# A new queue order for the FFN-up stretch of a one-core decoder layer (GpSimd transfer behind two products)

## The chip, the cores and the metric

One Trainium2 chip, one core. The metric is the device time in microseconds (us), the median of several runs. A profile is one execution of the same program with the hardware profiler on.

## What is computed

One decoder layer on 512 positions of width 1024, in fp32: two parallel mixers (sparse attention and gated DeltaNet), an output projection, a layer norm, a gated feed-forward network (FFN) with a width-3 causal convolution, and another layer norm. The change lies in the FFN alone:

```python
h = x @ w_up                       # 512 x 1024 @ 1024 x 5632, two branches of 2816 columns
h = causal_dwconv(h, conv_w)       # each column: its own 3 taps along the positions
a, b = split(h)                    # gate branch a, value branch b
f = (silu(a) * b) @ w_down         # 512 x 2816 @ 2816 x 1024
x = layer_norm(alpha * x + f)
```

## The kernel before

**Precision.** TensorE multiplies in fp32r, so every operand is split in two: a rounded copy `wh` (or `mh`, `sh`), made by ScalarE, and the rest `wl` = raw - `wh` (`ml`, `sl`), made by VectorE. A product is then three matmuls: `mh`·`wh`, `ml`·`wh`, `mh`·`wl`. For every weight block the way is therefore: a transfer into `raw` on SyncE's queue (SP), ScalarE's copy into `wh`, VectorE's subtraction into `wl`, TensorE's matmuls. `raw`, `wh` and `wl` have three buffers each.

**FFN-up** runs over 22 groups p of 128 columns, each with two branches (b = 0, the gate, and b = 1).
- A plain group (`plain`, lines 1553 to 1570) loads `raw` (L1557), splits it (L1561 ScalarE, L1562 VectorE), and runs matmuls of 512 columns into the PSUM tiles `pu0` and `pu1` (L1567).
- The seven odd groups 5, 7, ... 17 (`seven`, lines 1474 to 1539) replace eight half-size products by seven (a Strassen scheme) with matmuls of 256 columns (L1514) into `px` and `pz`, out of loads `raw` and `raw7` (L1492 to L1499; `raw7` has one buffer) and their splits (L1503 ScalarE, L1504 VectorE). Their results are joined in `wf0` and `wf1` by ScalarE (L1523, L1528, L1531, L1538) and VectorE (L1526, L1533, L1536).
- `gated` (L1541) then makes `fa0` or `fa1`: ScalarE takes `pu` or `wf` out with the last tap (L1544), VectorE adds the other two (L1547, twice). After it come tanh on ScalarE into `fth` (L1605), VectorE (L1606), and the product `fth` x `fa1` on GpSimd (L1607). Last, `fth` is split for FFN-down (ScalarE L1611 and L1618 into `pha`, VectorE L1612 and L1619 into `pla`), and sums of its halves are made (`sr`, VectorE L1613 and L1620 to L1622). `fth` has three buffers, `fa0` and `fa1` two each.

**FFN-down** uses the same scheme. The sums of `w_down` that it needs are made in DRAM by eight transfers that add to `wsum`, issued on GpSimd's queue by `sums` (L538), one or two after each of seven groups. They run beside FFN-up.

**What sets the order.** The program is written in a plain order, and every engine's queue is then put in the order of a table written out by hand, `QUEUES` (L138 to L343): for PE, DVE (VectorE), Activation (ScalarE), Pool (GpSimd) and SP a list of instruction numbers in the order in which that engine is to run them. `queues` (L346) ties each instruction to the one ahead of it. Each engine runs its list strictly in that order; an instruction that waits holds up all behind it.

Names below carry a number for each tile. `pu0_5920` and `pu1_5984` are those of group 8, `fth_5860` and `fth_5911` of groups 6 and 7. `px1_5939`, `pz1_5941`, `wf0_5942` and `wf1_5943` belong to group 9, `pu1_6220` to group 10, `px0_6175`, `pz1_6177` and `wf0_6178` to group 11, `pu0_6392` with `raw_6393` to group 12, and `raw7_6416` to group 13.

The lines that make and use the product and the splits around it:

```python
A.activation(acc, ps, AF.Copy, scale=w[:, 2:3])                                    # L1544
A.activation(hi, r, AF.Copy)                                                       # L1561
V.tensor_tensor(lo, r, hi.bitcast(F32), op=OP.subtract)                            # L1562
A.activation(th, g[0], AF.Tanh, scale=0.5)                                         # L1605
V.scalar_tensor_tensor(th, th, 1.0, g[0], op0=OP.add, op1=OP.mult)                 # L1606
G.tensor_tensor(th, th, g[1], op=OP.mult)                                          # L1607
A.activation(ph.j(j, bs), both, AF.Copy)                                           # L1618
i = G.dma_start(out=wsum[to], in_=src, **({"accum_op": OP.add} if add else {}))    # L538
```

Of the kernel before, what the change touches and what calls it, by code (L numbers as in the profile page):

```python
# [70 lines left out]
def layout(a):  # L71
# [149 lines left out]
2775-2778 2784-2785 2779 2786-2787 2780-2781 2794 2788-2790 2795-2797 2791 2798 2792 2799-2803 2806-2808 2804 2793  # L221
2809-2812 2805 2813-2829 2842-2843 2854 2844-2845 2830-2833 2846 2834 2847-2848 2835 2849-2850 2855 2851 2836 2856
2852 2857 2853 2837 2858 2838 2859-2860 2839-2841 2861-2868 2890 2869-2870 2878 2871-2872 2891 2873 2879 2874-2877
2880-2886 2892-2896 2902 2897-2899 2887 2900-2901 2888-2889 2903-2908 2914 2909 2915 2910 2916 2911 2917 2926
2912-2913 2918 2927 2919-2921 2928-2932 2938 2933-2934 2939 2922-2923 2940-2942 2924-2925 2943-2946 2935 2947 2936
2948 2937 2949-2956 2962 2957-2959 2963 2960-2961 2964-2967 2974 2968-2969 2986-2987 2970 2975-2978 2971 2988-2989
2972 2990 2973 2979-2985 2998 2991 2999 2992-2993 3000-3002 2994-2995 3003 2996 3004-3005 3010-3012 3006-3007 2997
3008-3009 3022 3013-3017 3023-3024 3018 3025 3019-3020 3034 3026 3035-3036 3021 3027-3029 3037-3038 3030-3031 3039
3032 3040 3046 3033 3041-3042 3047-3049 3043-3044 3058 3045 3050-3053 3059-3061 3054-3057 3062 3070 3063-3067 3071
3068 3072-3075 3082 3069 3076 3083 3077 3084 3078-3079 3094-3095 3080 3085 3096 3081 3086-3087 3097-3100 3088-3089  # L230
3101 3090-3093 3106-3109 3102-3105 3110-3114 3118-3123 3115-3117 3124 3130 3125-3126 3131-3138 3127-3128 3142
3139-3140 3143-3144 3141 3154 3129 3155 3145-3146 3166 3147 3156 3148 3157-3158 3149-3153 3167 3159-3160 3168-3170
# [73 lines left out]
1237 1249 1230 1250 1252 1255 1251 1257-1258 1243 1261 1260 1263-1264 1246 1265 1253 1267 1266 1268 1273 1254 1222
1256 1259 1278 1269 1279 1282 1271 1283 1270 1288 1272 1262 1274 1293 1289 1292 1284 1280 1276 1294-1295 1286 1290
# [35 lines left out]
145-146 144 147-155 157-172 156 173-186 188 190 192 194-201 187 202 191 193 203 189 204-205""",  # L343
}
# [1421 lines left out]
```

## Time and profile before

| | |
|---|---|
| median of 3 runs | 828.61 us (827.09 to 830.98) |
| the profiled execution | 827.81 us |
| its span, first to last instruction | 826.0 us (1.81 lie outside it) |
| TensorE (PE) busy | 803.1 us, 97% of the span |
| VectorE (DVE) busy | 630.6 us, 76% |
| ScalarE (ACT) busy | 432.1 us, 52% |
| GpSimd (POOL) busy | 192.7 us, 23% |
| mean granted clock of TensorE | 0.993 |
| DMA | 139.80 MB, mean 169 GB/s |

In a timeline a row gives the start, the duration, the engine, the line and the tile written and read; in square brackets stands how long the engine had been idle before it, and which instruction ended that. Matmuls overlap: the next starts well before the last one's end. FFN-up fills the span from some 490 to 740 us.

### The profile page before, as it was taken

The numbers are of one execution on the slowest core, as the hardware profiler recorded it, in microseconds if no ns is written. First come the engines' busy times: TensorE is split into PE (matmuls) and PEld (weight loads), VectorE is DVE, ScalarE is ACT, GpSimd is POOL, SyncE is SP. The second block draws the span as 40 slices with busy tenths as digits, with TensorE's granted clock in tenths as the row PEclk, the third lists the DMA queues.
The fourth block names the chain that finished last, engine by engine and source line by source line (L and its number), as shares of the span: only waits on it lengthen the run. The fifth ranks groups of instructions, "written<-read, shape, count | busy, mean of one in ns | idle before, by whom it ended". The sixth has DMA issues, their size and how long they took to land. (4 is left out here: it accounts for less than half of the span.)

```text
span 826.0 us, 12475 instructions
## 1 busy us (share of the span) xinstructions
PE 803.1 (97%) x4390; PEld 680.1 (82%) x4390; DVE 630.6 (76%) x1391; ACT 432.1 (52%) x965; POOL 192.7 (23%) x186
## 2 busy tenths in 40 slices
PE   9999999999999999999899999989999999999996
PEld 8788888788788888888787998878798888887884
DVE  5666689969678965555569969867788967888797
ACT  4452687774576764322354336544555644665641
POOL 0334716042265211332200112220101221100001
PEclk9999999999999999999999999999999999999998
DMA  8233326857245936546666697799348467566664
GB/s 280 85 112 110 100 62 203 164 184 155 75 128 137 192 91 153 153 128 153 242 237 207 233 200 244 170 238 212 108 141 280 141 145 187 164 198 215 187 206 152
DMA packets 53406, 139.80 MB, mean 169 GB/s; under 512 B 3936, under 2 KB 5088, under 8 KB 53088
## 3 DMA queue, kind: packets, MB, share of 16 engines
q1 hardware_dynamic: 36064, 92.88, 34.6%
q0 software_dynamic: 17280, 46.14, 24.5%
q8 instruction: 34, 0.56, 0.3%
q14 instruction: 28, 0.23, 0.1%
HBM read 136.91 MB, written 48.23 MB: 224 GB/s over the span
## 5 line engine op out<-in xcount | busy, mean ns | idle before, releaser
L494 PE MATMUL gps<-xh,wh 128*128 128x512 f32 x320 | 124.5, 399 | 2.6 <-ACT mt L1146 2.3
L497 PE MATMUL gps<-xh,wl 128*128 128x512 f32 x320 | 123.6, 397 | 0.0
L496 PE MATMUL gps<-xl,wh 128*128 128x512 f32 x320 | 123.4, 395 | 0.0
L1567 PE MATMUL pu<-mh,wh 128*128 128x512 f32 x208 | 80.8, 399 | 3.5 <-ACT wh L1561 3.5
L1567 PE MATMUL pu<-mh,wl 128*128 128x512 f32 x208 | 80.2, 399 | 1.8 <-DVE wl L1562 1.7
L1607 POOL TENSOR_TENSOR fth<-fth,fa 128x512 f32<-128x512 f32 x22 | 31.9, 1451 | 209.6 <-DVE fth L1606 146.8
L1567 PE MATMUL pu<-ml,wh 128*128 128x512 f32 x208 | 80.1, 397 | 0.0
L494 PEld LDWEIGHTS gps<-xh,wh 128*128 128x128 f32 x320 | 59.9, 188 | 14.1 <-issue 3.1
L497 PEld LDWEIGHTS gps<-xh,wl 128*128 128x128 f32 x320 | 60.2, 188 | 11.7 <-POOL wl L484 0.6
L496 PEld LDWEIGHTS gps<-xl,wh 128*128 128x128 f32 x320 | 60.2, 189 | 10.5
L484 DVE TENSOR_TENSOR wl<-raw,wh 128x512 fp32r<-128x512 f32 x66 | 46.9, 716 | 24.1 <-PE gps L497 13.2
L1469 ACT ACTIVATE wh<-raw 128x512 fp32r<-128x512 f32 x67 | 40.4, 627 | 38.7 <-DMA raw<-wsum 13.0
L1562 DVE TENSOR_TENSOR wl<-raw,wh 128x512 fp32r<-128x512 f32 x52 | 39.1, 754 | 22.2 <-ACT wh L1561 12.3
L1470 DVE TENSOR_TENSOR wl<-raw,wh 128x512 fp32r<-128x512 f32 x67 | 45.3, 705 | 13.7 <-ACT wh L1469 13.4
L1561 ACT ACTIVATE wh<-raw 128x512 fp32r<-128x512 f32 x52 | 32.7, 629 | 40.5 <-PE pu L1567 34.2
L1503 ACT ACTIVATE wh<-raw 128x512 fp32r<-128x512 f32 x49 | 30.8, 630 | 39.6 <-PE px L1514 13.7
L1547 DVE SCALAR_TENSOR_TENSOR fa<-pu,fcw,fa 128x511 f32<-128x511 f32 (+1 forms) x60 | 44.3, 745 | 8.7 <-ACT fa L1544 8.6
L1567 PEld LDWEIGHTS pu<-mh,wh 128*128 128x128 f32 x208 | 39.8, 192 | 10.1 <-ACT wh L1561 3.9
L1567 PEld LDWEIGHTS pu<-mh,wl 128*128 128x128 f32 x208 | 39.9, 192 | 9.8 <-DVE wl L1562 3.1
L480 ACT ACTIVATE wh<-raw 128x512 fp32r<-128x512 f32 x46 | 28.8, 627 | 35.3 <-PE gps L496 23.7
L484 POOL TENSOR_TENSOR wl<-raw,wh 128x512 fp32r<-128x512 f32 x30 | 40.4, 1347 | 24.0 <-DVE wh L482 9.4
L1567 PEld LDWEIGHTS pu<-ml,wh 128*128 128x128 f32 x208 | 39.8, 191 | 6.5
(498 smaller groups left out, 2229.6 us busy)
## 6 DMA issues: line engine op xcount, KB each, us to landing
raw<-in_wT SPq DMA_DIRECT2D x40, 512.0 KB, 3.6
raw<-in_up SPq DMA_DIRECT2D x37, 512.0 KB, 4.6
wsum<-in_down POOLq DMA_DIRECT2D x6, 2816.0 KB, 22.4
usum<-in_up POOLq DMA_DIRECT2D x6, 1792.0 KB, 16.0
raw<-wsum SPq DMA_DIRECT2D x20, 512.0 KB, 3.9
raw<-in_down SPq DMA_DIRECT2D x15, 512.0 KB, 3.8
osum<-in_wo POOLq DMA_DIRECT2D x6, 1024.0 KB, 11.3
wsum<-wsum POOLq DMA_DIRECT2D x2, 2816.0 KB, 14.6
```

What stands on the lines that cost most here:

```text
L484: eng.tensor_tensor(wl, r, wh.bitcast(F32), op=OP.subtract)
L494: i = PE.matmul(ps, wh[k], mh_(k), start=(k == 0), stop=False)
L496: PE.matmul(ps, wh[k], ml_(k), start=False, stop=False)
L497: PE.matmul(ps, wl[k], mh_(k), start=False, stop=(k == n - 1))
L1469: A.activation(hi, raw[:, i], AF.Copy)
L1470: V.tensor_tensor(lo, raw[:, i], hi.bitcast(F32), op=OP.subtract)
L1503: E("uh", 10 * p + i, "A").activation(hi, r, AF.Copy)
L1547: V.scalar_tensor_tensor(acc[:, n:], ps[:, :S - n], w[:, i:i + 1], acc[:, n:], op0=OP.mult, op1=OP.add)
L1561: A.activation(hi, r, AF.Copy)
L1562: V.tensor_tensor(lo, r, hi.bitcast(F32), op=OP.subtract)
L1567: q = PE.matmul(ps, w[:, j], x[:, k, :], start=k == 0 and i == 0, stop=k == KD - 1 and i == 2, skip_group_check=True)
L1607: G.tensor_tensor(th, th, g[1], op=OP.mult)
```

## The change

No line of the program changes and no instruction is added or removed. The table `QUEUES` is made anew for all five queues in the stretch from about 545 to 700 us. In the Pool and SP tables:

```diff
     "Pool": ...
-133-134 111 135-138 140 139 141 150 142 151 143-145 157 146 148-149 160 147 152 163 153 156 154-155 158-159 161-162
-165-166 164 167-168 170-171 169 172-181""",
+133-134 111 135-138 140 139 141 150 142 151 143-145 157 146 148-149 160 147 152 163 153 156 155 154 158-159 161-162
+165 164 167 166 168 170-171 169 172-181""",
-    "SP": """0-7 17 8-9 15 25 10 12 11 13-14 19 18 16 20-22 24 23 26-75 81 78 77 82 79 83 76 84 80 85-129 132 130-131 133-143
+    "SP": """0-7 17 8-9 15 25 10 12 11 13-14 19 18 16 20-22 24 23 26-75 81 78 77 82 79 83 76 84 80 85-115 118 116-117 119-123 125
...
```

On SP three short loads of `raw` (L1499) move one or two places ahead of loads of `raw7`, and one L1496 load moves two places ahead. The tables of PE, DVE and Activation differ in many places of the stretch; the ones that matter below are these.

GpSimd's queue, all of its difference (`fth` products and `wsum` transfers):

```order
 L1607 TENSOR_TENSOR fth_5675<-fth_5675,fa1_5671 128x512
 L1607 TENSOR_TENSOR fth_5911<-fth_5911,fa1_5907 128x512
+L1607 TENSOR_TENSOR fth_5860<-fth_5860,fa1_5856 128x512
 L538 DMA wsum0_100<-in_down 1408x1x512
-L1607 TENSOR_TENSOR fth_5860<-fth_5860,fa1_5856 128x512
 L1607 TENSOR_TENSOR fth_6096<-fth_6096,fa1_6092 128x512
 L1607 TENSOR_TENSOR fth_6147<-fth_6147,fa1_6143 128x512
...
 L1607 TENSOR_TENSOR fth_6383<-fth_6383,fa1_6379 128x512
 L1607 TENSOR_TENSOR fth_6619<-fth_6619,fa1_6615 128x512
-L538 DMA wsum3_103<-wsum2_102 1408x512
 L1607 TENSOR_TENSOR fth_6568<-fth_6568,fa1_6564 128x512
 L1607 TENSOR_TENSOR fth_6804<-fth_6804,fa1_6800 128x512
+L538 DMA wsum3_103<-wsum2_102 1408x512
```

The transfer into `wsum0` now comes behind both products instead of between them, and the one into `wsum3` behind two more products.

ScalarE's queue after the tanh of group 7, at about 549 us (place A below), first as it is before, then as changed:

```order
L1605 ACTIVATE fth_5911<-fa0_5903 128x512
L1618 ACTIVATE pha_5439<-fth_5911 128x2x256
L1544 ACTIVATE fa0_5980<-pu0_5920,fcw_324 128x512
L1561 ACTIVATE wh_6159<-raw_6157 128x512
L1611 ACTIVATE pha_5439<-fth_5860 128x256
L1544 ACTIVATE fa1_6092<-pu1_5984,fcw_324 128x512
```

```order
L1605 ACTIVATE fth_5911<-fa0_5903 128x512
L1544 ACTIVATE fa0_5980<-pu0_5920,fcw_324 128x512
L1618 ACTIVATE pha_5439<-fth_5675 128x2x256
L1538 ACTIVATE wf0_5942<-px1_5939 128x256
L1544 ACTIVATE fa1_6092<-pu1_5984,fcw_324 128x512
L1561 ACTIVATE wh_6159<-raw_6157 128x512
```

The split of `fth_5911` no longer stands ahead of the weight copy `wh_6159`, and four other copies do. Of these, `fa1_6092` goes into the buffer of `fa1_5907`, which GpSimd's product `fth_5911` reads. On VectorE's queue the sum `wf1_5943` (L1536), which frees `pz` for the matmuls of about 566 us (place B), stood behind `wl_6260`; changed, it stands here:

```order
L1606 SCALAR_TENSOR_TENSOR fth_5911<-fth_5911,fa0_5903 128x512
L1562 TENSOR_TENSOR wl_6160<-raw_6157,wh_6159 128x512
L1620 TENSOR_TENSOR sr0a_5441<-fth_5860,fth_5911 128x256
L1547 SCALAR_TENSOR_TENSOR fa0_5980<-pu0_5920,fcw_324,fa0_5980 128x511
L1536 TENSOR_TENSOR wf1_5943<-wf1_5943,pz1_5941 128x256
L1504 TENSOR_TENSOR wl_6183<-raw7_6180,wh_6182 128x512
```

It moved thirteen places ahead. At about 579 us (place C) TensorE goes from group 10 to group 12, with half-size products of group 11 between. Its queue there, first as it is before, then as changed:

```order
L1514 MATMUL pz1_6177<-sh3_5460,wl_6340 128x256
L1514 MATMUL px0_6175<-mh_4006,wl_6359 128x256
L1567 MATMUL pu0_6392<-mh_4006,wh_6395 128x512
L1567 MATMUL pu0_6392<-ml_4007,wh_6395 128x512
L1567 MATMUL pu0_6392<-mh_4006,wl_6396 128x512
```

```order
L1567 MATMUL pu1_6220<-mh_4006,wl_6313 128x512
L1514 MATMUL px0_6175<-ml_4007,wh_6358 128x256
L1567 MATMUL pu0_6392<-mh_4006,wh_6395 128x512
L1567 MATMUL pu0_6392<-ml_4007,wh_6395 128x512
L1514 MATMUL pz1_6177<-sh3_5460,wl_6340 128x256
```

Most half-size products of group 11 now follow the first two matmuls of `pu0_6392` instead of preceding them. ScalarE's queue at the same place, before and changed:

```order
L1538 ACTIVATE wf0_6178<-px0_6175 128x256
L1561 ACTIVATE wh_6395<-raw_6393 128x512
L1544 ACTIVATE fa1_6328<-pu1_6220,fcw_324 128x512
L1503 ACTIVATE wh_6418<-raw7_6416 128x512
```

```order
L1544 ACTIVATE fa0_6216<-pu0_6156,fcw_324 128x512
L1544 ACTIVATE fa1_6328<-pu1_6220,fcw_324 128x512
L1561 ACTIVATE wh_6395<-raw_6393 128x512
L1611 ACTIVATE pha_5439<-fth_6096 128x256
L1538 ACTIVATE wf0_6178<-px0_6175 128x256
```

The copy `fa1_6328`, which needs all of `pu1_6220`, has moved from behind the weight copy `wh_6395` to ahead of it. On VectorE its tap follows it, ahead of the two splits that the half-size products need:

```order
L1547 SCALAR_TENSOR_TENSOR fa1_6328<-pu1_6220,fcw_324,fa1_6328 128x511
L1504 TENSOR_TENSOR wl_6340<-raw7_6292,wh_6339 128x512
L1504 TENSOR_TENSOR wl_6359<-raw_6356,wh_6358 128x512
```

Before, the same tap stood ten places or more behind both splits.

## Rows read from the trace of the kernel before

**Rows 1.** Busy time by stretch. Columns: the stretch, its length, then for each engine its busy time and instructions (PE, PEld, DVE, ACT, POOL), the granted clock of TensorE (1.00 is full), the busy share of the DMA engines, GB/s.

```profile
540.00:560.00 20.00, 16.39 (x87) 13.60 (x87) 11.26 (x19) 9.07 (x18) 4.25 (x3) 0.91 0.96 234
560.00:580.00 20.00, 18.35 (x117) 16.16 (x116) 15.39 (x26) 8.87 (x18) 1.41 (x2) 1.00 0.94 230
580.00:600.00 20.00, 18.97 (x104) 16.39 (x105) 14.90 (x25) 10.89 (x21) 2.46 (x2) 0.91 0.24 76
...
620.00:640.00 20.00, 20.00 (x128) 18.05 (x127) 16.75 (x29) 10.89 (x20) 3.47 (x3) 1.00 0.84 289
```

**Rows 2.** What TensorE waited for between 495 and 720 us: all of it. Columns: the waiting matmul and what ended the wait, us in total, times, the longest.

```profile
PE pu L1567 <- ACT wh L1561: 3.5, 2, 2.5
PE pu L1567 <- DVE wl L1562: 1.7, 2, 1.1
PE pz L1514 <- DVE wf L1536: 1.0, 1, 1.0
```

**Rows 3.** The timeline at place A, 548.6 to 555.1 us.

```profile
548.66 0.63 ACT L1605 ACTIVATE fth<-fa 128x512 f32<-128x512 f32 x1 [1.65 <-DVE sr1a L1621]
...
550.17 1.27 POOL L1607 TENSOR_TENSOR fth<-fth,fa 128x512 f32<-128x512 f32 x1 [19.81 <-DVE fth L1606]
...
550.32 0.28 PE L1514 MATMUL px<-ml,wh 128*128 128x256 f32 x1
...
550.44 0.28 PE L1514 MATMUL px<-mh,wl 128*128 128x256 f32 x1
551.38 1.73 POOL L538 DMA_DIRECT2D wsum<-in_down  x1
551.47 0.63 ACT L1618 ACTIVATE pha<-fth 128x512 fp32r<-128x512 f32 x1 [2.17 <-POOL fth L1607]
552.00 0.67 ACT L1544 ACTIVATE fa<-pu,fcw 128x512 f32<-128x512 f32 x1
552.28 2.13 POOL L1607 TENSOR_TENSOR fth<-fth,fa 128x512 f32<-128x512 f32 x1
552.57 0.62 ACT L1561 ACTIVATE wh<-raw 128x512 fp32r<-128x512 f32 x1
553.22 1.75 DVE L1562 TENSOR_TENSOR wl<-raw,wh 128x512 fp32r<-128x512 f32 x1 [3.20 <-ACT wh L1561]
...
553.24 0.50 PE L1567 MATMUL pu<-mh,wh 128*128 128x512 f32 x1 [2.53 <-ACT wh L1561]
...
555.03 0.79 PE L1567 MATMUL pu<-mh,wl 128*128 128x512 f32 x1 [1.05 <-DVE wl L1562]
```

**Rows 4.** The timeline at place B, 565 to 567 us.

```profile
565.46 0.69 DVE L1562 TENSOR_TENSOR wl<-raw,wh 128x512 fp32r<-128x512 f32 x1 [0.27 <-ACT wh L1561]
566.07 0.41 DVE L1536 TENSOR_TENSOR wf<-wf,pz 128x256 f32<-128x256 f32 x1
...
566.63 0.36 PE L1514 MATMUL pz<-sh,wh 128*128 128x256 f32 x1 [1.00 <-DVE wf L1536]
```

**Rows 5.** The timeline at place C, 579 to 582 us.

```profile
579.07 0.28 PE L1514 MATMUL px<-mh,wl 128*128 128x256 f32 x1
...
579.67 0.62 ACT L1561 ACTIVATE wh<-raw 128x512 fp32r<-128x512 f32 x1
579.88 1.28 POOL L1607 TENSOR_TENSOR fth<-fth,fa 128x512 f32<-128x512 f32 x1 [0.78 <-DVE fth L1606]
...
580.32 1.39 DVE L1562 TENSOR_TENSOR wl<-raw,wh 128x512 fp32r<-128x512 f32 x1 [0.52 <-ACT wh L1561]
...
580.34 0.50 PE L1567 MATMUL pu<-mh,wh 128*128 128x512 f32 x1 [0.99 <-ACT wh L1561]
...
581.64 0.74 DVE L1547 SCALAR_TENSOR_TENSOR fa<-pu,fcw,fa 128x510 f32<-128x510 f32 x1
...
581.77 0.50 PE L1567 MATMUL pu<-mh,wl 128*128 128x512 f32 x1 [0.69 <-DVE wl L1562]
```

**Rows 6.** Busy time by stretch, columns as in Rows 1: behind place A, behind place C, and around a wait at 396 us, ahead of FFN-up.

```profile
554.00:559.00 5.00, 3.97 (x11) 3.17 (x12) 4.04 (x7) 2.38 (x6) 0.42 (x1) 0.66 0.99 160
582.00:586.00 4.00, 4.00 (x13) 3.19 (x13) 3.61 (x7) 1.76 (x3) 0.00 (x0) 0.57 0.00 0
396.00:399.00 3.00, 0.72 (x4) 0.32 (x3) 2.47 (x5) 1.07 (x2) 1.85 (x2) 1.00 0.37 89
```

**Rows 7.** The timelines of GpSimd and of VectorE at an earlier `wsum` transfer.

```profile
524.52 1.73 POOL L538 DMA_DIRECT2D wsum<-in_down  x1
...
524.89 0.43 DVE L1622 TENSOR_TENSOR sr3a<-sr1a,fth 128x256 f32<-128x256 f32 x1
```

**Rows 8.** Transfers. Issue, number, size of one, and median us from issue to landing: first the `wsum` transfer of 551 us, then loads of 622 to 638 us, while another `wsum` transfer runs, then loads of 640 to 662 us, where none runs. The last row is that of the `raw7` loads of L1492 alone.

```profile
wsum<-in_down POOLq DMA_DIRECT2D x1, 2816.0 KB, 23.2
...
raw<-in_up SPq DMA_DIRECT2D x2, 512.0 KB, 5.7
...
raw<-in_up SPq DMA_DIRECT2D x1, 256.0 KB, 6.9
...
raw<-in_up SPq DMA_DIRECT2D x4, 512.0 KB, 4.2
...
raw<-in_up SPq DMA_DIRECT2D x1, 256.0 KB, 3.3
...
DMA to landing us min/median/max: 4.0/4.3/5.2
```

More of the change, by code (lines that the diff above doesn't have):

```diff
@@ new lines @@
+3230-3231 3250 3232-3235 3251 3236-3237 3239-3249 3252 3262-3263 3253-3254 3264 3255-3257 3265-3267 3258 3268-3271
+3259-3261 3272 3274-3280 3286-3291 3273 3281-3285 3292 3298 3293-3294 3299 3295 3300-3301 3296-3297 3302-3303
+3310-3312 3304-3306 3322 3307-3309 3313-3321 3323 3334 3324 3335 3325-3327 3336-3337 3328-3330 3338 3331-3332 3339
+3333 3346-3350 3358-3359 3340-3341 3360-3361 3342 3362 3343-3344 3363-3366 3345 3351-3357 3370-3374 3382-3383
+3367-3368 3384 3369 3375-3381 3394-3396 3385-3388 3397-3399 3389-3392 3400-3404 3393 3405-3417 3430 3418 3431
@@ new lines @@
+3419-3421 3432-3434 3422 3435-3438 3423 3439 3424 3440 3425-3427 3441 3428-3429 3442-3450 3454 3451-3453 3466
+3455-3458 3467 3459-3460 3468-3471 3478-3479 3472-3473 3461 3474-3476 3462-3464 3477 3465 3480-3485 3502 3486-3488
+3503-3510 3489-3490 3511 3491 3512 3492-3494 3513-3514 3495 3515 3496-3497 3516-3520 3498-3499 3526 3521 3527-3529
+3522 3530-3532 3500 3533 3501 3534 3523 3535-3538 3524 3539-3540 3550-3551 3541-3543 3552 3525 3544-3547 3553-3556
+3548-3549 3557-3564 3574 3565-3566 3575-3576 3567-3568 3577 3569-3571 3578 3572 3579-3581 3573 3582-3586 3598-3600
@@ new lines @@
+3587-3589 3601-3607 3590-3591 3608-3611 3592-3593 3622 3612 3623 3613 3624 3594-3596 3625-3627 3614 3628-3630
+3615-3616 3597 3631-3634 3617 3635-3636 3618-3620 3646-3647 3637-3639 3621 3640-3644 3648-3649 3645 3650-3659 3670
+3673 3671 3674 3672 3660-3661 3675 3679 3662-3663 3676 3680 3677 3681 3678 3685 3664 3686 3665 3682 3687 3666-3668
+3691-3692 3683 3693 3669 3684 3697-3699 3688-3689 3703-3705 3690 3694-3696 3700-3702 3709-3711 3706-3708 3715
+3712-3713 3716-3717 3721-3722 3739 3736 3714 3718 3723 3740 3719-3720 3724 3741 3727 3737 3745-3747 3738 3742-3744
@@ new lines @@
+3728 3725 3729 3751-3752 3726 3753 3748-3750 3733 3730-3731 3754-3758 3760 3759 3763-3765 3761-3762 3766-3768 3734
+3769-3770 3772 3771 3773 3775-3776 3774 3735 3778 3777 3779-3782 3732 3783-3785 3787-3789 3786 3790 3802 3805
+3791-3794 3806-3807 3803-3804 3795 3808-3810 3814-3815 3799 3811-3812 3796 3813 3816-3818 3800 3819 3797 3823 3798
+3824 3820 3825 3821-3822 3826 3829-3830 3801 3831 3827-3828 3832-3834 3838 3835 3839 3836 3840 3837 3841-3847 3850
+3848-3849 3851 3853 3871-3872 3852 3856 3854 3873 3855 3877 3868 3859 3857-3858 3869 3862 3878-3879 3860-3861 3870
@@ new lines @@
+3874-3876 3880-3881 3883-3885 3882 3865 3889-3890 3886 3866 3887-3888 3892 3891 3895-3896 3863-3864 3867 3893-3894
+3897 3901-3903 3907-3908 3898 3909 3899-3900 3904-3906 3910-3916 3919 3937 3934 3917 3938-3939 3920 3918 3935
+3922-3924 3936 3921 3943 3925-3927 3940-3941 3931 3928 3942 3944 3929 3946 3945 3932-3933 3949 3930 3950-3951 3947
+3955-3956 3948 3957 3952-3953 3961-3963 3954 3967 3958-3960 3968 3964 3969 3973 3965-3966 3974-3975 3970-3971
+3979-3980 3972 3981 3976-3978 3982 4000 3983-3984 4001 3985 3988 3986-3987 3989-3990 3994 3991-3993 3997 3995 4002
```

99 lines of the change are left out of this document (37 added, 62 removed).

## The prediction

> **What bounds the kernel now.** I first read the waits and the busy time by stretch. In the stretch that the change touches TensorE is the bound: from 620 to 640 us it is busy 20.00 of 20.00 us, even with the DMA engines at a share of 0.84 [rows 1]. So work moved on another engine counts only where TensorE has to wait. It does so in three places between 495 and 720 us, and the list of its waits there is complete: 3.5 us for ScalarE's `wh`, 1.7 for VectorE's `wl`, 1.0 for VectorE's `wf` [rows 2], 6.2 in all. The timelines tell why.
>
> *Place A, 550.6 to 555.0 us.* `pu` of group 10 needs `wh` (L1561), which ScalarE ends at 553.19. Ahead of it on ScalarE stands the split L1618 of `fth_5911`, which waits until 551.47 for GpSimd's product, begun at 550.17. TensorE waits 2.53. GpSimd's `wsum` transfer takes the queue at 551.38 for 1.73 us, and so the second product lasts from 552.28 to 554.41, the time in which VectorE makes `wl`: 1.75 us for what takes 0.69 elsewhere [rows 3, 4]. TensorE waits another 1.05. *Place B:* `wf1` (L1536) ends 566.48, since it stands behind a `wl` begun at 565.46, and TensorE waits 1.00 [rows 4]. *Place C:* 0.99 for `wh`, then 0.69 for a `wl` that ran 1.39 us beside a product [rows 5].
>
> Second, the clock. Behind A the granted clock is 0.66 over 5 us, behind C 0.57 over 4 us [rows 6]: TensorE ran at 1.2 instead of 2.4 GHz for most of that. It lost 5 x 0.34 = 1.7 us and 4 x 0.43 = 1.7 us. So the most that the change can give in these places is 6.2 + 3.4 = 9.6 us, 1.2% of the time.
>
> **The change, part by part.** The instructions are the same, so each term is a wait that goes, comes or changes size. I count what TensorE lost by its starts: two 256-column matmuls start 0.12 apart [rows 3], and I take 0.24 for 512 columns.
>
> *Place A, first wait.* ScalarE ends the tanh L1605, begun at 548.66, as now. Then come `fa0_5980` and the split of `fth_5675`, whose product is long done. `wf0_5942` needs the last `px` matmul, 550.44 + 0.28 = 550.72, and so ends by about 551.1. `fa1_6092` writes the buffer that the product `fth_5911` reads, and starts at that product's end, 551.47. One ScalarE start later (552.00 to 552.57 gives 0.57) `wh_6159` begins at 552.04. It ends 0.62 later, and TensorE resumes at 552.70 instead of 553.24: 0.54 earlier. The wait is not gone. Only one of the two operations between GpSimd's product and `wh` is.
>
> *Place A, second wait.* The second product now follows the first at once and runs 551.45 to 552.73 (1.28, as at 579.88 [rows 5]). So `wl_6160`, begun at 552.72, runs beside no product and takes 0.69: 553.41. TensorE goes on at about 553.46, against 555.03. Place A as a whole gives **-1.57 us**, of which the transfer's move makes 1.03.
>
> What does the transfer now run beside? Its issue (1.73) falls to 552.73 to 554.46, beside `wl_6160` and two or three more VectorE instructions. The trace has one such issue beside a busy VectorE: at 524.52 it took 1.73, the same as at 551.38 beside an idle one, and VectorE's L1622 inside it took 0.43 [rows 3, 7]. From below I therefore take 0; from above it costs `wl_6160` the 1.06 us that the product cost it. I take 0, since row and case agree in kind. The Trainium skill speaks against this move: its page "SBUF — State Buffer", section "SBUF: two separate sides", says that GpSimd cannot write a transfer's descriptors while VectorE holds the port that they share, so a transfer issued beside a busy VectorE would run late. No run here shows it so far: the two equal issues speak against it, and with it the sum would be that of the third rival below.
>
> *Place B.* `wf1_5943` now stands thirteen places earlier on VectorE, ahead of two splits that TensorE needs before it. The wait falls away: **-1.0**. Its cost to `wl_6183` behind it, 0.41, is covered: TensorE has nine or more matmuls of group 10 to do in between.
>
> *Place C* gets a new order, with a new wait. `fa1_6328` now stands ahead of `wh_6395` on ScalarE, and it needs the last matmul of `pu1_6220`, which TensorE issues two matmuls before it needs `wh_6395`. From the start of that last matmul: 0.40 until its result is there, 0.57 for `fa1_6328`, 0.62 for `wh_6395` and two hand-overs of 0.03 make 1.65, less the 0.35 that TensorE is busy with it and with the next: 1.3 lost (now 1.15: from 579.07 + 0.12 to 580.34 [rows 5]). Next, the tap of `fa1_6328` (0.74) stands ahead of `wl_6340` on VectorE: about 0.3. Then `wl_6359` comes 0.15 late. Last, the load L1492 of `raw7_6416` can only go out when `wl_6340` has read the one `raw7` buffer: its landing in 4.3 (4.0 to 5.2) [rows 8], the copy of 0.62 and a hand-over of 0.1 make 5.05, while TensorE has 20 half and 9 full matmuls in between, 20 x 0.12 + 9 x 0.24 = 4.55, and 0.05 of the last wait's slack: about 0.45. In sum 2.2. Now it is 1.15 + (581.77 - 580.34 - 0.48 = 0.95) = 2.1. So **+0.1**; from below -0.4 (the last two hidden), from above +1.9 (the load at 5.2, and the product beside `wl_6340`, which made 1.39 of 0.69 [rows 5] here and up to 1.75 at A).
>
> *The `wsum3` transfer and SP's three short loads.* They are moved within stretches where TensorE never waits. I take 0; the price if they collide is in the fourth rival.
>
> *The clock.* TensorE lost 2.7 + 1.3 us within 4.6 us at A, and 2.1 within 2.6 us at C, and both times the clock fell. At 396 us it stood idle for 3.00 - 0.72 = 2.28 us in one go and the clock stayed at 1.00 [rows 6]. After the change A loses 2.4 us in one stretch of 2.9, near the case without a fall, and C 2.2 spread over seven. So neither is decided by rows: from below both falls go (-3.4), from above both stay (0). I take one gone: **-1.7**. The skill's page "TensorE: Matmul & The Clock Gate", Part 1, says that the number of slow matmuls of one and the same kernel varies from run to run; no row here shows a second run.
>
> Sum against the profiled execution: 827.81 - 1.57 - 1.0 + 0.1 - 1.7 = 823.64. The median of the runs lies 0.80 above that execution (828.61 against 827.81), so I forecast **824.4 us**, 0.5% faster.
>
> **The rivals.**
> 1. *Both falls of the clock stay* (A and C each still a loss of over 2 us): 824.4 + 1.7 = 826.1. For it: both fell at losses of 2.1 and more. Against: 396 us.
> 2. *No fall is left*: 824.4 - 1.7 = 822.7.
> 3. *The waits come back at C.* The transfer, issued 1.35 us later, still lands some 23 us after its issue [rows 8], at about 576, and so runs into the loads of 574.5 on which the loop through `raw7` hangs. C then costs its upper end, +1.9 instead of +0.1, and both falls stay: 826.1 + 1.8 = 827.9, no change. It decides from a landing of 4.5 us on.
> 4. *Slower: the `wsum3` transfer collides at 642 us.* It is issued behind two more products, so no longer at 622 but at about 642 us, and runs until 656, beside three groups of loads that now have the queues to themselves. Loads beside such a transfer landed in 5.7 (512 KB) and 6.9 (256 KB) instead of 4.2 and 3.3 [rows 8]. If no load there had slack: 1.5 + 3.6 + 1.5 = 6.6 us, and one more fall of 1.7: 824.4 + 8.3 = 832.7, 0.5% slower. It decides where the slack is under 1.5 us. Against it: with the same transfer at 622 to 637 TensorE was busy 20.00 of 20.00 [rows 1].
>
> **How the numbers follow.** A measurement of this kernel tells about 0.5%, 4.1 us, from no change: faster is below 824.5, slower above 832.8. One fall gone, 824.4: chance 0.42; rival 1, 0.18; rival 2, 0.14; rival 3, 0.14; rival 4, 0.12. The first lies at the bound: half of it counts as faster, with rival 2 and a sixth of rival 1: 0.21 + 0.14 + 0.03 = 0.38. Half of rival 4 and a little for what I don't see make slower 0.08. The rest, 0.54, is within 0.5%. The range goes from rival 2 less the 0.4 from C's lower end and 0.8 for a median that lies at the profile's time, 821.5, to rival 3 with the 1.06 of a slowed `wl_6160`, 829.0. It leaves out rival 4 and some of the edges.
>
> **What would show it.** Right: at A one wait for `wh` of about 2.0 us and next to none for `wl`, TensorE on `pu` of group 10 some 1.6 us earlier, and the two products of 1.28 us end to end with the transfer behind them. At B no wait for `wf`. At C a wait of about 1.2 for `wh`, then small ones for the half-size products' `wl` and for the `raw7` load. From 600 to 740 us 20.00 of 20.00. Wrong: a product still beside `wl_6160`; waits for DMA between 642 and 660; a clock below 1.00 behind both places, or behind neither; a C of 3 us or more.

## The result, and the profile after

| | before | changed |
|---|---|---|
| median | 828.92 us (10 runs, 827.01 to 830.98) | 824.97 us (10 runs, 821.55 to 826.06) |
| ratio | | 0.9947, 95% interval 0.9929 to 0.9964 |
| the profiled execution | 827.81 us | 826.06 us |
| its span, mean granted clock | 826.0 us, 0.993 | 824.3 us, 0.994 |

The change makes the kernel 0.5% faster (the interval does not reach 1); 824.4 was forecast. The waits of TensorE between 495 and 720 us, all of them, in the same view as [rows 2]:

```profile
PE pu L1567 <- ACT wh L1561: 3.2, 2, 2.0
PE px L1514 <- ACT wh L1503: 0.6, 1, 0.6
```

They were 6.2 us and are 3.8. The wait for `wl` at A and that for `wf` at B are gone, C's two have become a longer one and a new one for the `raw7` copy. The timeline of place A, to be laid beside [rows 3]:

```profile
551.23 2.50 POOL L1607 TENSOR_TENSOR fth<-fth,fa 128x512 f32<-128x512 f32 x2 [19.82 <-DVE fth L1606]
552.54 0.69 ACT L1544 ACTIVATE fa<-pu,fcw 128x512 f32<-128x512 f32 x1 [0.33 <-POOL fth L1607]
553.12 0.62 ACT L1561 ACTIVATE wh<-raw 128x512 fp32r<-128x512 f32 x1
553.67 1.73 POOL L538 DMA_DIRECT2D wsum<-in_down  x1
553.78 0.69 DVE L1562 TENSOR_TENSOR wl<-raw,wh 128x512 fp32r<-128x512 f32 x1 [2.69 <-ACT wh L1561]
553.80 0.50 PE L1567 MATMUL pu<-mh,wh 128*128 128x512 f32 x1 [2.01 <-ACT wh L1561]
554.52 0.50 PE L1567 MATMUL pu<-mh,wl 128*128 128x512 f32 x1
```

The two products now run end to end (x2, 2.50 us), the transfer follows, `wl` takes 0.69, and the `wl` matmul at 554.52 has no wait. All of this execution is 1.07 us late against the one of before when it comes to A (VectorE's L1606 on `fth_5911` at 550.40 against 549.33; it had lost 1.7 us to a fall of the clock at 398 us, shown below), so that matmul is 555.03 + 1.07 - 554.52 = 1.58 us earlier. Place C, beside [rows 5]:

```profile
574.70 0.28 PE L1514 MATMUL px<-ml,wh 128*128 128x256 f32 x1
574.96 0.69 ACT L1544 ACTIVATE fa<-pu,fcw 128x512 f32<-128x512 f32 x1 [1.18 <-PE pu L1567]
575.54 0.62 ACT L1561 ACTIVATE wh<-raw 128x512 fp32r<-128x512 f32 x1
576.22 0.50 PE L1567 MATMUL pu<-mh,wh 128*128 128x512 f32 x1 [1.24 <-ACT wh L1561]
576.35 1.29 DVE L1504 TENSOR_TENSOR wl<-raw,wh 128x512 fp32r<-128x512 f32 x2
576.56 0.40 PE L1567 MATMUL pu<-ml,wh 128*128 128x512 f32 x1
577.08 0.39 PE L1514 MATMUL pz<-sh,wl 128*128 128x256 f32 x1
577.10 0.33 SPq L1492 DMA_DIRECT2D raw<-in_up  x1
...
581.80 0.63 ACT L1503 ACTIVATE wh<-raw 128x512 fp32r<-128x512 f32 x1 [1.53 <-DMA raw<-in_up]
...
582.49 0.39 PE L1514 MATMUL px<-mh,wh 128*128 128x256 f32 x1 [0.56 <-ACT wh L1503]
```

ScalarE's copy out of `pu1_6220` stands ahead of `wh`, and TensorE waits 1.24 for the two in a row. The `raw7` load goes out at 577.10, when VectorE has read the buffer, and the copy of what it brings starts as it lands. By stretch, as in [rows 1] and [rows 6]:

```profile
580.00:600.00 20.00, 19.43 (x118) 16.91 (x117) 14.50 (x25) 11.21 (x21) 2.91 (x2) 1.00 0.49 155
...
640.00:660.00 20.00, 20.00 (x128) 17.88 (x127) 16.18 (x28) 11.18 (x21) 2.75 (x3) 1.00 0.85 288
...
554.00:559.00 5.00, 5.00 (x16) 3.73 (x16) 4.70 (x10) 2.75 (x5) 1.40 (x1) 0.66 0.56 70
```

One of the two falls of the clock is left, behind A (0.66 over 5 us). From 640 to 660, where the moved `wsum3` transfer now runs, TensorE is busy 20.00 of 20.00. Ahead of FFN-up, where nothing was moved, stands the wait at 396 us of [rows 6]. It is the same, but here the clock fell behind it: the waiting matmul, and the stretch behind it, first of the changed kernel and then of the kernel before:

```profile
397.85 0.48 PE L494 MATMUL gps<-xh,wh 128*128 128x512 f32 x1 [2.28 <-ACT mt L1146]
```

```profile
398.00:402.00 4.00, 4.00 (x11) 3.13 (x11) 2.02 (x5) 3.27 (x7) 0.00 (x0) 0.57 0.93 347
398.00:402.00 4.00, 3.33 (x15) 2.77 (x16) 3.26 (x9) 3.97 (x8) 0.00 (x0) 1.00 0.93 332
```

### The profile page after: what moved, and what is told of

Same layout as the page of the kernel before. It is cut to its first block, busy times and chain, and to the rows that moved or that the text cites. A ratio compares the mean times of both kernels' runs of the same rounds, so it can differ in the third digit from the quotient of the medians.

```text
span 824.3 us, 12473 instructions
## 1 busy us (share of the span) xinstructions
PE 803.4 (97%) x4390; PEld 680.3 (83%) x4390; DVE 629.1 (76%) x1391; ACT 432.1 (52%) x965; POOL 192.0 (23%) x186
## 4 chain that ended last, share of the span: by engine, by line
PE 83%; DVE 6%; DMA 5%; ACT 4%; issue 1%; SPq 0%; POOL 0%; ACTq 0%; DVEq 0%; POOLq 0%
PE pu L1567 16%; PE gps L494 9%; PE gps L496 9%; PE gps L497 9%; PE px L1514 4%; PE px L1644 3%; PE pz L1514 3%; PE pout L1114 2%; PE aps L1100 2%; PE pz L1644 2%; PE pm L496 2%; PE pm L497 2%; PE pm L494 2%; DMA raw<-wsum 2%; PE dps L684 2%; DMA raw<-in_down 1%
## 5 line engine op out<-in xcount | busy, mean ns | idle before, releaser
L484 DVE TENSOR_TENSOR wl<-raw,wh 128x512 fp32r<-128x512 f32 x66 | 47.0, 718 | 23.4 <-PE gps L497 13.2
L1470 DVE TENSOR_TENSOR wl<-raw,wh 128x512 fp32r<-128x512 f32 x67 | 45.8, 710 | 14.2 <-ACT wh L1469 13.9
L1562 DVE TENSOR_TENSOR wl<-raw,wh 128x512 fp32r<-128x512 f32 x52 | 36.4, 702 | 19.4 <-ACT wh L1561 14.0
L1547 DVE SCALAR_TENSOR_TENSOR fa<-pu,fcw,fa 128x511 f32<-128x511 f32 (+1 forms) x60 | 44.2, 744 | 8.5 <-ACT fa L1544 8.3
L1504 DVE TENSOR_TENSOR wl<-raw,wh 128x512 fp32r<-128x512 f32 x49 | 35.4, 727 | 15.6 <-ACT wh L1503 14.8
```

Of the source, the lines that this page charges most:

```text
L484: eng.tensor_tensor(wl, r, wh.bitcast(F32), op=OP.subtract)
L1470: V.tensor_tensor(lo, raw[:, i], hi.bitcast(F32), op=OP.subtract)
L1504: E("ul", 10 * p + i).tensor_tensor(lo, r, hi.bitcast(F32), op=OP.subtract)
L1547: V.scalar_tensor_tensor(acc[:, n:], ps[:, :S - n], w[:, i:i + 1], acc[:, n:], op0=OP.mult, op1=OP.add)
```

## The experiments

**A measure that leaves the noise out.** Heads of the runs differ (up to 485 us these profiles lie between 0.5 us ahead of and 1.8 behind that of before), and so do their ends in FFN-down. Nine of the 14 profiles have the fall at 398 us; less that fall, the heads, which are the same instructions, still spread over 1.2 us. So beside the runs' ratio I use the stretch in which the order changes: from the start of VectorE's L1606 on `fth_5911` to that on `fth_7508` (group 19). (`fth_5911` is group 5's: the numbers that the kernel's description, the prediction and the expectations give to the groups of the tiles at places A to C are two too high. No time rests on them.) "Clock" is the time lost in it to the low clock, the sum of 2 x (1 - granted clock) over windows of 2 us; "rest" is the stretch without it. A fall comes out as 1.70 us, but the one behind A in e2 as twice that (granted clock 0.51 from 556 to 563 us). Each stretch is one execution, and no kernel was profiled twice, so a few tenths of a us between two rests tell nothing. A ratio is to runs of the kernel before on the same chip. It stands on ten to twelve runs, in e8 on eight, in e5 and e13 on six, in e6 on five, in e9 on four.

| kernel | ratio to before, interval | stretch, from - to | clock | rest |
|---|---|---|---|---|
| before | 1 | 154.12 (549.33 - 703.45) | 3.40 | 150.72 |
| changed | 0.9947, 0.9929 to 0.9964 | 150.55 (550.40 - 700.95) | 1.70 | 148.85 |
| e1 | 0.9970, 0.9954 to 0.9986 | 153.38 (550.02 - 703.40) | 3.40 | 149.98 |
| e2 | 1.0012, 0.9998 to 1.0025 | 152.89 (551.13 - 704.02) | 3.42 | 149.47 |
| e12 | 0.9977, 0.9963 to 0.9991 | 151.39 (550.25 - 701.64) | 1.70 | 149.69 |
| e3 | 0.9971, 0.9958 to 0.9983 | 152.20 (549.36 - 701.56) | 1.70 | 150.50 |
| e7 | one run, 827.12 us | 152.47 (550.97 - 703.44) | 0 | 152.47 |
| e4 | 0.9955, 0.9941 to 0.9968 | 149.54 (550.09 - 699.63) | 1.70 | 147.84 |
| e5 | 0.9921, 0.9902 to 0.9941 | 147.81 (550.99 - 698.80) | 0 | 147.81 |
| e6 | 0.9918, 0.9897 to 0.9938 | 146.68 (550.67 - 697.35) | 0 | 146.68 |
| e8 | 0.9949, 0.9927 to 0.9971 | 149.36 (548.79 - 698.15) | 0 | 149.36 |
| e9 | 0.9906, 0.9883 to 0.9928 | 146.75 (549.49 - 696.24) | 0 | 146.75 |
| e10 | 0.9980, 0.9964 to 0.9996 | 144.62 (550.69 - 695.31) | 0 | 144.62 |
| e13 | 0.9913, 0.9894 to 0.9932 | 147.19 (549.13 - 696.32) | 0 | 147.19 |

### The parts of the change, alone and undone

**e1: the wsum0 transfer alone, in the order of before.** On GpSimd's queue:

```diff
 L1607 fth_5911<-fth_5911,fa1_5907
+L1607 fth_5860<-fth_5860,fa1_5856
 L538 DMA wsum0_100<-in_down
-L1607 fth_5860<-fth_5860,fa1_5856
```

> The kernel before, with one step of the change alone: on GpSimd's queue the wsum0 transfer behind the second product. Theory (the transfer held back the second product, and the product held back VectorE's wl): at A the products end to end, wl 0.69 instead of 1.75 us, TensorE's second wait 1.05 -> under 0.1, its first wait 2.5 unchanged; 828.9 - 1.0 = 827.9 with the clock's falls as before, 826.2 if the fall behind A goes. Rival (the transfer's issue itself holds back VectorE): wl stays at 1.4 to 1.8 us, second wait 0.7 or more, time 828.9.

Its timeline at A:

```profile
550.86 2.49 POOL L1607 TENSOR_TENSOR fth<-fth,fa 128x512 f32<-128x512 f32 x2 [19.82 <-DVE fth L1606]
...
553.29 1.72 POOL L538 DMA_DIRECT2D wsum<-in_down  x1
553.92 0.69 DVE L1562 TENSOR_TENSOR wl<-raw,wh 128x512 fp32r<-128x512 f32 x1 [3.20 <-ACT wh L1561]
553.94 0.50 PE L1567 MATMUL pu<-mh,wh 128*128 128x512 f32 x1 [2.53 <-ACT wh L1561]
```

`wl` takes 0.69 in the middle of the transfer's issue (553.29 to 555.01), so it was the product and not the issue that had stretched it. The first wait stays 2.53, the second is gone. The rest shrinks by 0.74, and the runs say 0.9970: the mechanism of the theory holds. The runs gained some 2.5 us, more than its 1.0; their mean granted clock was higher too (0.9936 against 0.9922, about 1.1 us less of lost time).

**e2: the sum `wf1_5943` early, alone, in the order of before; e12: e1 and e2 together.** On VectorE's queue:

```diff
 L1620 sr0a_5441<-fth_5860,fth_5911
+L1536 wf1_5943<-wf1_5943,pz1_5941
 L1504 wl_6183<-raw7_6180,wh_6182
...
 L1562 wl_6260<-raw_6257,wh_6259
-L1536 wf1_5943<-wf1_5943,pz1_5941
```

> The kernel before, with one step of the change alone: VectorE's sum wf1_5943 (L1536) twelve places earlier. Theory: the wait for wf at B (1.00 us) is gone, A and C as before, 828.9 - 1.0 = 827.9. Rival (what TensorE gains at B it waits for at C, since C hangs on VectorE and GpSimd and not on TensorE): the wait at B is gone, those at C grow from 1.7 to 2.5 or more, time 828.9.

> The kernel before with the steps of e1 and e2 together. e2 took B's wait away and its stretch was 1.2 us shorter in the profile, but the runs were not faster (ratio 1.0012). Theory (the stretch is what the change makes, and the runs of e2 lost it outside): the stretch from group 7's tanh product to group 19's 1.7 to 2.2 us shorter than before, runs 1.0 us under e1's: ratio 0.996. Rival (B's wait is covered and its end is worth nothing): the same ratio as e1, 0.997, or above, and a stretch that is 0.7 to 1.0 us shorter.

TensorE's waits in e12 between 495 and 720 us (e2 has the same, without the last and with A's 1.1 for `wl`):

```profile
PE pu L1567 <- ACT wh L1561: 3.5, 2, 2.5
PE pu L1567 <- DVE wl L1562: 0.7, 1, 0.7
PE pz L1514 <- ACT wh L1503: 0.4, 1, 0.4
PE px L1514 <- ACT wh L1503: 0.2, 1, 0.2
```

The wait for `wf` (1.00) is gone in both, but 0.4 to 0.6 of it comes back as waits for the next weight copy. C is as it was, so e2's rival is wrong; e12's has its numbers right (0.9977, and a rest 1.03 below that of before). In worth the two runs disagree: the rest shrinks by 1.25 us in e2 but by 0.29 from e1 to e12, and the runs show no gain (1.0012; 0.9977 against e1's 0.9970). In the old order B is worth between nothing and 1 us, and these runs don't settle it.

**e3: the transfer back between the two products, in the changed order** (e1's diff the other way round).

> The changed kernel with the wsum0 transfer put back between the two products. Theory: at A the second product lasts 2.1 us again, wl_6160 1.7, a second wait of about 1 us; the loads of 557 to 560 land as late as they do in the changed kernel; 825.0 + 1.0 = 826, up to 827.5 if the clock falls behind A more often. Rival (the loss at A is covered by the late loads behind it, as A's first wait was in e4): the wait comes, but the stretch stays within 0.4 us, 825.

Its timeline at A:

```profile
552.31 2.13 POOL L1607 TENSOR_TENSOR fth<-fth,fa 128x512 f32<-128x512 f32 x1
552.74 2.27 DVE L1562 TENSOR_TENSOR wl<-raw,wh 128x512 fp32r<-128x512 f32 x1 [2.69 <-ACT wh L1561]
552.76 0.50 PE L1567 MATMUL pu<-mh,wh 128*128 128x512 f32 x1 [2.01 <-ACT wh L1561]
...
555.06 0.59 PE L1567 MATMUL pu<-mh,wl 128*128 128x512 f32 x1 [1.56 <-DVE wl L1562]
```

`wl` takes 2.27 us, TensorE's second wait is back and longer than before (1.56), and the rest grows by 1.65. The ratio goes from 0.9947 to 0.9971, 2 us, with intervals that overlap. The theory holds, and by the trace the transfer's place is worth even more in the changed order than the 1.03 of my sum: `wh` is earlier there, and `wl` meets more of the product.

**e7: the wsum3 transfer back to its old place (here 623 us), in the changed order.** One run alone, so its time is not compared.

```diff
 L1607 fth_6619<-fth_6619,fa1_6615
+L538 DMA wsum3_103<-wsum2_102
 L1607 fth_6568<-fth_6568,fa1_6564
 L1607 fth_6804<-fth_6804,fa1_6800
-L538 DMA wsum3_103<-wsum2_102
```

> The changed kernel with the wsum3 transfer put back two products earlier, to about 621 us. Theory (its place costs and gives nothing): TensorE busy 20.00 of 20.00 from 600 to 680 us, as in the changed kernel, time 822 to 826. Rival (its place matters): a wait of 0.5 us or more there, or one less in FFN-down.

TensorE's waits at two places of e7's timeline:

```profile
569.11 0.38 PE L1514 MATMUL px<-sh,wh 128*128 128x256 f32 x1 [1.45 <-ACT wf L1528]
...
638.54 0.39 PE L1514 MATMUL px<-sh,wh 128*128 128x256 f32 x1 [1.60 <-ACT wf L1528]
```

The short loads of 618 to 642 us (issue, number, size, median us to landing), of e7 and then of the changed kernel:

```profile
raw<-usum SPq DMA_DIRECT2D x2, 256.0 KB, 8.3
raw<-in_up SPq DMA_DIRECT2D x1, 256.0 KB, 8.9
```

```profile
raw<-usum SPq DMA_DIRECT2D x2, 256.0 KB, 2.9
raw<-in_up SPq DMA_DIRECT2D x1, 256.0 KB, 3.2
```

The theory is wrong, the rival holds. Beside the transfer the short loads (L1496 to L1499) land in 8 to 9 us instead of 3, ScalarE's next weight copy waits for one, its L1528 stands behind that copy, and TensorE waits 1.60 for L1528. In the order of before the same place had cost nothing [rows 1]: the short loads landed in some 7 us there, and no wait followed. Which of the other moves used up that slack was not tried. So this move, which I priced at nothing, keeps a wait of 1.6 us out of the changed order. The wait at 569 us belongs to the next part.

### What bounds the stretch behind place A

**e4: place A opened.** ScalarE's queue, and on VectorE's `sr0a_5441` behind `wl_6183`:

```diff
 L1605 fth_5911<-fa0_5903
+L1561 wh_6159<-raw_6157
 L1544 fa0_5980<-pu0_5920,fcw_324
 L1618 pha_5439<-fth_5675
 L1538 wf0_5942<-px1_5939
 L1544 fa1_6092<-pu1_5984,fcw_324
-L1561 wh_6159<-raw_6157
```

> The changed kernel, with place A's remaining wait taken out: ScalarE makes wh_6159 right behind the tanh of group 7, ahead of the four copies, and VectorE's sr0a_5441 goes behind wl_6183. Theory (the wait of 2.0 us for wh is that of a weight copy that stands behind a copy that needs GpSimd's product): the wait at A falls to 0.3 or less, no fall of the clock behind it, 825.0 - 1.7 - 1.2 (the fall, seen in some seven of ten runs) = about 822. Rival (A is bound by the load or by the product all the same): another wait of 1 us or more at A or within the next 4 us, for wl or for the next group's wh, time 824 to 825.

TensorE's two longest waits there between 495 and 720 us, and then ScalarE's row ahead of the longest:

```profile
PE px L1514 <- ACT wf L1528: 2.0, 1, 2.0
PE pu L1567 <- ACT wh L1561: 1.2, 1, 1.2
```

```profile
565.97 0.63 ACT L1503 ACTIVATE wh<-raw 128x512 fp32r<-128x512 f32 x1 [3.44 <-DMA raw<-usum]
```

A's wait of 2.0 is gone, and a wait of 2.0 for L1528 has come at 567 us: ScalarE stood idle for 3.44 us, until a load of `usum` landed. The rest gains 1.0, the runs nothing clear (0.9955 against 0.9947). The rival holds, in a form that I hadn't written down: not A, but the short loads of 555 to 560 us bound this stretch. (The "seven of ten runs" of the expectation is a guess from the runs' mean clocks: only one of the ten was profiled. Here the clock did not fall behind A, but behind C.)

**e8: e4, with the wsum0 transfer four products later (about 595 us).**

> e4 (A opened) with the wsum0 transfer another four products later, at about 596 us. Theory (the loads of 557 to 560 us land in 7 to 10 us only because they run beside that transfer): they land in 4 to 6, the wait of 2.0 for L1528 falls to 0.3 or less, the waits between 545 and 580 fall from 3.4 to 1.5 (those of C alone), and the clock stays at 1.00: 824.4 - 2.0 - 1.5 = 821. Rival (the loads are late by their own order on the queue): landings within 2 us of those in e4, the wait stays, 824.4.

Landings of the loads of L1496 to L1499 at 554 to 561 us (columns as above), first in e4, then in e8:

```profile
raw<-usum SPq DMA_DIRECT2D x2, 256.0 KB, 8.2
raw<-in_up SPq DMA_DIRECT2D x1, 256.0 KB, 9.9
```

```profile
raw<-usum SPq DMA_DIRECT2D x2, 256.0 KB, 3.1
raw<-in_up SPq DMA_DIRECT2D x1, 256.0 KB, 3.8
```

The landings fall to 3.1 and 3.8, further than the theory says, and with them the wait at 567. But the transfer carries the wait along: at 610.85 TensorE waits 1.51 us for L1528, now of the next half-size group. The time (0.9949, 824.3 us) is that of e4, not the 821 expected. So the loads were late by the transfer beside them, and moving it by one group moves the wait by one group.

### Better orders

**e5: place C mended.** On ScalarE's queue `wh_6395` ahead of `fa1_6328`; on VectorE's:

```diff
 L1606 fth_6096<-fth_6096,fa0_5980
+L1504 wl_6340<-raw7_6292,wh_6339
 L1533 wf1_6179<-wf1_6179,px0_6175
+L1504 wl_6359<-raw_6356,wh_6358
 L1606 fth_6147<-fth_6147,fa0_6139
 L1547 fa0_6216 (first tap)
 L1547 fa1_6328 (first tap)
-L1504 wl_6340<-raw7_6292,wh_6339
-L1504 wl_6359<-raw_6356,wh_6358
```

> The changed kernel, with place C's order mended: ScalarE's wh_6395 ahead of fa1_6328, and VectorE's wl_6340 and wl_6359 ahead of the tanh product and the taps. Theory: C's first wait 1.24 -> about 0.3 (wh_6395 then hangs on the buffer that pu1_6220's matmuls free), the raw7 load goes out 3 us earlier and its wait of 0.56 goes; 825.0 - 1.6 = 823.4, the clock behind A as before. Rival (the loops move the waits on): waits of 1.5 us or more in sum between 574 and 600, time 825.

Three of TensorE's rows in its timeline, and the row of 554 to 559 us in its table of stretches:

```profile
554.39 0.50 PE L1567 MATMUL pu<-mh,wh 128*128 128x512 f32 x1 [2.01 <-ACT wh L1561]
568.99 0.39 PE L1514 MATMUL px<-sh,wh 128*128 128x256 f32 x1 [1.31 <-ACT wf L1528]
575.49 0.50 PE L1567 MATMUL pu<-mh,wh 128*128 128x512 f32 x1 [0.24 <-ACT wh L1561]
```

```profile
554.00:559.00 5.00, 4.61 (x24) 3.72 (x25) 4.63 (x9) 3.35 (x6) 1.99 (x2) 1.00 0.43 55
```

C's waits fall to 0.24, the `raw7` wait is gone, and the runs gain (0.9921 against 0.9947, some 2.2 us; the 1.6 of the theory lies within the intervals). And look at A: the same wait of 2.01 as in the changed kernel, but the clock stays at 1.00 behind it, and then L1528 makes TensorE wait 1.31 at 569. In the changed kernel's profile the clock fell, TensorE came 1.7 us later, and the same load was in time. e7 shows it too: no fall, and 1.45 at 569. The fall and the wait for the load stand in for each other.

**e6: e4 and e5 together.**

> e4 and e5 together: A opened and C mended. e4 showed that TensorE, 2.0 us earlier behind A, waited 2.0 us at 567 us for px, since ScalarE's L1528 stood behind a weight copy that waited for a load beside the wsum transfer. Theory (that load bounds the stretch, not A): no gain over e5 from opening A, waits of some 3 us in all between 550 and 580 (2.0 or more of them for L1528), 821.6 within a us. Rival (A's gain stands, e4 only lost it to a fall of the clock): 1.5 us or more below e5, 820.

0.9918 against e5's 0.9921: opening A adds nothing that the runs can tell, as the theory says, though the rest falls by 1.1. L1528's wait is 1.4 there and all waits from 550 to 580 are 1.9, not the 2.0 and 3 that I expected.

**e9, e10, e13: e6, with the wsum0 transfer at 593, 692 and 648 us.** On GpSimd's queue it goes behind `fth_6383`, behind `fth_7423`, and behind `fth_6855`.

> A opened, C mended and the wsum0 transfer at about 596 us: e6 and e8 together. Theory: next to no wait of TensorE between 545 and 620 us (under 1 us), no fall of the clock: 821 less C's 1.5 = 819.5, the fastest of all. Rival (the late transfer hits the loads at 596 to 620, where TensorE never waited): waits of 1 us or more there, 821 or more.

> A opened and C mended as in e9, and the wsum0 transfer still later, at about 692 us, behind the half-size groups. e9 left one wait of 1.7 us at 600 to 620, where that transfer now ran. Theory (the transfer costs a wait wherever the short loads of a half-size group run beside it, and next to nothing beside plain groups): under 0.6 us of waits from 545 to 720, span some 1.5 us below e9's: 819. Rival (at 692 it hits FFN-down's first loads, or isn't done when they read wsum0 at 725): waits of 1 us or more from 692 on, 820.5 or more.

> A opened and C mended, and the wsum0 transfer issued at about 642 us, right behind the first wsum3 transfer on GpSimd's queue, so that it runs from about 650 on: behind the last short loads (645 us) and ahead of FFN-down's first ones (689 us), which e10 hit. Theory (a transfer costs nothing beside plain groups' loads): under 0.6 us of waits from 545 to 720, a stretch 1.5 us shorter than e9's, 819. Rival (two transfers at once are more than the loads of 644 to 660 stand): waits of 1 us or more between 640 and 690, or in FFN-down because the last wsum3 transfer ends later, 821 or more.

The longest waits of e9, of e10 and of e13 between 495 and 725 us:

```profile
PE px L1514 <- ACT wf L1528: 1.7, 1, 1.7
```

```profile
PE px L1644 <- ACT wh L1469: 3.6, 2, 1.8
```

```profile
PE pu L1567 <- DVE wl L1562: 1.5, 1, 1.5
PE pu L1567 <- ACT wh L1561: 1.0, 2, 0.7
```

GpSimd's next transfer in e13, the second into `wsum3`:

```profile
673.65 1.73 POOL L538 DMA_DIRECT2D wsum<-in_down  x1 [12.65 <-DVE wl L1562]
```

Each place has its price. In e9 it is 1.7 us at 609, beside the next short loads. In e10 it is 3.6 us at 704 to 709, where loads of 512 KB for FFN-down landed in 9.7 us, and the clock then fell (0.57 from 705 to 713 us, 3.4 us of lost time). In e13 it is 0.7 at 660, beside plain groups' loads, and 1.5 at 680, in a way that no expectation names. The transfer issued at 647.54 landed 25.8 us later, at 673.34; GpSimd stood idle for 12.65 us and issued its next transfer at 673.65. The product queued behind it ran from 674.56 to 676.71 beside two of VectorE's L1547, which took 4.08 us instead of 1.5, and the `wl` behind them came late. So the two transfers never ran at once: GpSimd, and what stood behind it, waited for the first.

e10 has the shortest stretch of all (144.62) and gives it back behind it (0.9980). e9 has the lowest ratio (0.9906, 820.5 us, four runs), but e13 (0.9913), e6 and e5 lie inside its interval: these runs don't tell the four apart. All three theories were too hopeful about the waits. The rivals have the waits right, in e13 for another reason; of the times, only e10's rival is right (e9's 820.5 lies between 819.5 and 821, e13's 820.2 below its rival's 821).

## Why the prediction was right, and where it was not

The time (824.4 for 824.97) and the sign were right, at the bound of what can be told from no change. At 592 us (VectorE's L1606 on `fth_6332`: 592.37 against 595.29) the changed profile had gained 2.92 + 1.07 = 3.99 us; the sum said 4.17. The 3.99 are 1.58 at A, 1.70 from the clock and about 1.0 at B, less 0.3 at C. By 704 it was 3.57: 0.4 went in steps too small for the list of waits. From there to the end of the span it took 0.8 us more than the one profile of before (824.3 - 700.95 against 826.0 - 703.45); the medians, of ten runs each, differ by 3.95. SP's loads and most of the other moves were not tried alone. What the changed kernel has over e12 (0.9947 against 0.9977) is 1.0 us less of waits on the lists and a higher mean clock of the runs (0.9950 against 0.9933, some 1.4 us).

- **Place A: right.** First wait 2.01 (1.98 worked out), the second gone, 1.58 us in all (1.57). e1 and e3 show that the transfer's place makes the second wait, and that VectorE slows beside the product, not beside the issue. The rule of the Trainium skill that speaks against the move ("SBUF — State Buffer", "SBUF: two separate sides": VectorE can keep GpSimd from writing descriptors) did not decide here; the page ties it to VectorE operations in a two-port mode, and no run here shows whether these are such. The issue took 1.73 beside a busy VectorE as it did beside an idle one, and the transfer landed in 24.0 us against 23.2.
- **Place B: right in the changed kernel, but not by itself.** The 1.00 that I took came out nearly whole: the list of waits has nothing between A and C, and TensorE lost only 0.2 us there, ahead of `px0_6175` at 568.73. But in e2 and e12 0.4 to 0.6 of it turned into a wait for the next weight copy, and their runs show no gain. The step "the wait falls away: -1.0" asked what stands behind `wf1` on VectorE, and not what TensorE needs next from ScalarE. That the changed order has no such wait was not worked out.
- **Place C: right in kind, a little small.** Counted by TensorE's starts, as the prediction does, it lost 1.40 (574.70 + 0.12 to 576.22), then 0.28 for `wl_6340` (576.56 + 0.24 to 577.08), then 0.72 for the `raw7` load (581.53 + 0.24 to 582.49): 2.4 in all, where I had 2.2 (1.3, 0.3, 0.15 and 0.45). So the term was +0.3 and not +0.1. (In the last part 5.05 and 4.55 should read 5.02 and 4.56, which changes nothing.) e5 shows that this was the price of the order and not of the work: without it the runs are at 0.9921.
- **The clock: the number came out, half by luck.** One fall of two went, 1.70 us. Over all runs the mean granted clock went from 0.9922 (29 runs, taken beside e1) to 0.9950 (10): 6.4 us of lost time against 4.1. But a wait does not decide a fall. The wait at 396 us, which I held against the falls at A and C, is 2.28 us in all 14 profiles. The clock fell behind it in nine, the changed kernel's among them, and in five it did not; I had seen one of the five. A's wait of 2.0 was followed by a fall in the changed kernel and by none in e5 and e7; A's 2.5 alone by one in e1 and by none in e12. C's 0.99 + 0.69 was followed by one in before, e1 and e12, and by none in e2; C's new 1.24 by one in e4 and by none in the changed kernel, e3, e7 and e8. All three profiles with 3.6 us at A (before, e2, e3) fell. So the new order seems to make falls rarer, and which of them goes in one execution is chance. The Trainium skill's page "TensorE: Matmul & The Clock Gate", Part 1, says of a kernel's start that the number of slow matmuls varies from run to run; these profiles show the same in mid-kernel. What I missed: where A's clock doesn't fall, 1.3 to 1.5 us come back as a wait for the load (e5, e7). Rival 2 could therefore not have given its 1.7 in full.
- **The wsum3 transfer: 0 was the wrong price.** I argued that TensorE never waits there and priced only a collision at the new place. In the changed order the old place is the one that collides (e7: 1.60). Rival 4 was right about the loads and wrong about the wait: at 640 to 655 those of 256 KB landed in 6.9 to 7.0 us, and TensorE was busy 20.00 of 20.00. Its price for loads of 512 KB, 5.7, is the median of one beside the transfer (7.57) and one issued after that had landed (3.75). (This transfer copies `wsum2` into `wsum3`. Of the eight that the description calls adding, four copy and four add.)
- **Rival 3** didn't happen: the `raw7` load went out at 577.10, 0.6 us before the transfer landed, and took 4.6; C lost about 0.3 more than before, not 1.9.

## What to carry to other kernels

Work out a new order by walking each tight round trip from the instruction that releases it; that gave place A to 0.01 us. Before you book a wait that ends as a gain, ask which load or copy is next and how much slack it has: A's 2.0 us, taken out in e4, came back as another wait of 2.0, and B's 1.0, taken out alone in e2, shows no gain in the runs. A large transfer in the background is part of the order: it can cost a wait wherever short loads run beside it or a product stands behind its issue, and moving it moves that wait. And don't read a rule for the clock out of one execution.

## What was not expected of the hardware

Short loads landed two to three times as late beside a transfer in the background: 256 KB took 2.9 to 4.0 us alone (medians), and 7 to 10 us beside a transfer of 2816 KB on GpSimd's queue, one that adds (e4 against e8) or one that copies (e7 against the changed kernel). With one such transfer still on its way, GpSimd issued the next only 0.3 us after the first had landed, and stood idle until then (twice in e13, 8.4 and 12.65 us).

A fall of TensorE's clock in mid-kernel cost 1.70 us or twice that (behind A in e2, at 706 us in e10). Behind the same wait of 2.28 us, in the same instructions, it came in nine executions and not in five.
